# Context rows of the adaLN product moved from GpSimd to VectorE in the first stage of a hybrid attention layer

## The chip, the cores and the metric

The kernel runs on one core of a Trainium2 chip. The metric is the device time of one execution in microseconds (us); before the change it is 1164.74 us, the median of three runs (1163.18 to 1165.64). Lower is better.

## What is computed

One layer of a backbone over 1024 image tokens of width 1024, with 256 context tokens in front of them. What matters here is the start of it, cut from the reference:

```python
def modulate(x, cond, norm_g, w_ada, b_ada):
    shift, scale, gate = jnp.split(jax.nn.silu(cond) @ w_ada + b_ada, 3, axis=-1)
    ...
    return rms_norm(x, norm_g) * (1 + scale) + shift, gate

h, gate = modulate(x, c, lp['norm_g'], lp['w_ada'], lp['b_ada'])
hc, gate_c = modulate(xc, c_ctx, lp['norm_g'], lp['w_ada'], lp['b_ada'])
z = h @ lp['w_in']
kc, vc = na_kv(hc @ lp['w_in'][:, A_K:A_Z], lp['k_norm_g'])
```

So shift and scale are products of a vector (silu of the condition) with the 1024 x 1024 matrices of `w_ada`, once with the image's condition and once with the context's. Behind it come the projections of `z`, neighbourhood attention with context keys, two convolution branches, gates, and the output projection. Everything is float32; each matmul is made of three products of high and low parts.

## The kernel before, in words

The first stage walks over eight columns k of 128 channels. Tiles of 128 tokens of x (`xt`, 128 x 1024) are normed row by row (`normed`, L312 to L320: squares with a sum on ScalarE, the root on GpSimd by `rsqrt_mean`, L77 and L78, the scaling at L319 on VectorE). Tiles 0 to 3 are the first half of the image (`ha`, one tile per column), tiles 4 and 5 and later 6 and 7 the second half (`hb`); two context tiles follow.

For a column k the two rows of `w_ada` (scale and shift, 128 x 1024, 512 KB each) are loaded on SyncE's queue (`load_w_ada`, L300) and each is multiplied with the row of silu(c) and summed by one VectorE instruction (`image_ada`, L351, instruction at L355). Two tiny instructions then give the column's scale A (L357) and shift B (L358). In `modulated` (L322) TensorE transposes the tiles (L327), ScalarE writes the high part with A and B applied (L329) and the same value in full (`xh`, L332), and a subtraction makes the low part (L335). `outer` (L378) multiplies the column at once with the first weights of q, k and v, into six PSUM banks: L380 and L381 need the high part, L382 the low part. `second` (L386) does a column of tiles 4 and 5, three columns behind the first half (`LAG = 3`). `rest_image` (L420) does tiles 6 and 7; their products run inside `qkv` by `mm3` (L106 to L108). After that come the first gate (`glu_steps`, tile `gps`) and the context.

The same 16 rows of `w_ada` are needed with silu(c_ctx): `ctx_ada(i)`, L360, i = 2 x column + (0 scale, 1 shift). In the kernel before, rows 0 to 7 are done in two pieces inside the column loop: GpSimd multiplies (L368) and ScalarE sums (L370). Rows 8 to 15 are single VectorE instructions (L366), emitted behind the loop. The tables `W_POOL`, `LO_POOL` and `LO_POOL2` say which low parts of weights (`split_chunk`, L89) and of columns (L335) GpSimd makes. A scheduler orders the instructions of each engine; `tc.issue_after` holds a piece back until another one. Each engine then works its list in order.

`row4k` is a ring of 14 buffers (`ROWS`) of 4 KB per partition, for x tiles from number 3 on, `w_ada` rows from 6 on, the silu(c_ctx) row `sc1` and later weights; a load into it waits for the last reader of the buffer it reuses.

Of the kernel before, what the change touches and what calls it, by code (L numbers as in the profile page):

```python
# [8 lines left out]
F32 = mybir.dt.float32  # L9
F32R = mybir.dt.float32r  # L10
BF16 = mybir.dt.bfloat16
AF = mybir.ActivationFunctionType
ALU = mybir.AluOpType
# [4 lines left out]
P = 128  # L18
D = 1024
KT = 8  # L20
S = 1024
# [6 lines left out]
MASK_PAD = 1024  # L28
WARM = 10
NT = 2  # L30
ROWS = 14
LAG = 3
EARLY = 6
RAW1 = 6
CTX_AT = (8, 3, 3, 3)

LO_POOL, LO_POOL2, W_POOL = (7,), (4, 5, 6, 7), (0, 1, 2, 4, 5, 6)

CTX_ROWS = {0: 1, 1: 2, 2: 3, 3: 4, 4: 5, 5: 6, 6: 7, 7: 7}


@with_exitstack
def tile_hybrid(ctx: ExitStack, tc, x, xT, cx, cond, crow, ng, w_ada, b_ada, wqkv, wz,
                wout, wo, qg, kg, rpbs, mask, cs, cf, cfb, lng, lnb, out):
    nc = tc.nc
    pe, act, dve, pool = nc.tensor, nc.scalar, nc.vector, nc.gpsimd
# [22 lines left out]
    def const(src, shape, name):  # L69
        t = cst.tile(shape, F32, name=name)  # L70
        nc.sync.dma_start(t, src)
        return t


    def rsqrt_mean(dst, ss, n, k):

        pool.tensor_scalar(out=dst, in0=ss, scalar1=1.0 / n, scalar2=EPS, op0=ALU.mult, op1=ALU.add)  # L77
        pool.tensor_tensor(out=dst, in0=dst, in1=half_neg[:, :k], op=ALU.pow)  # L78


    def split_chunk(src, n, lo_eng, raw=None):
        wp = state["wp"]
        if raw is None:
            raw = wp.tile([P, 384], F32, tag="wr", name="wr", bufs=3)
            nc.sync.dma_start(raw[:, :n], src)
        hi = wp.tile([P, 384], F32R, tag="wh", name="wh")
        act.copy(hi[:, :n], raw[:, :n])  # L87
        lo = wp.tile([P, 384], F32R, tag="wl", name="wl")
        state["lo"] = lo_eng.tensor_tensor(out=lo[:, :n], in0=raw[:, :n], in1=hi[:, :n].bitcast(F32), op=ALU.subtract)  # L89
        return hi, lo  # L90

    def load_w(src, kts, lo_eng):
# [31 lines left out]
    B512 = [slice(0, 512), slice(512, 1024)]  # L124
    state = {"wp": wp}
# [103 lines left out]
    def hcols(part, k, sl):  # L229

        o = sl.start // 512
        return hlf[o][k][:, part, sl.start - o * 512 : sl.stop - o * 512]
    chd = dram.tile([KT, P, 2 * L], F32, name="chd")

    def tmp(name="tmp"):
        return rp.tile([P, 512], F32, tag="tmp", name=name)
# [29 lines left out]
    with tc.tile_pool(name="st", bufs=1) as st, tc.tile_pool(name="ps_t", bufs=1, space=PSUM) as pst:  # L266
# [6 lines left out]
        def row4k(name, dt=F32):  # L273
            return st.tile([P, D], dt, tag="row", name=name, bufs=ROWS)

        def four(t):
            return t.rearrange("p (a b n) -> p a b n", a=2, b=2)
# [9 lines left out]

        def silu_rows(i):

            r = row4k("sc1") if i else st.tile([P, D], F32, name="sc")  # L290
            for h in range(2):
                ps = pst.tile([P, 512], F32, tag="t", name="c_ps", bufs=NT)
                for k in range(4):
                    pe.transpose(out=ps[:, k * P : k * P + P], in_=cond_t[:, 4 * h + k, i : i + 1].broadcast_to([P, P]), identity=ident)
                if i:
                    act.copy(r[:, B512[h]], ps)
                else:
                    dve.tensor_copy(r[:, B512[h]], ps)
            return four(r)

        def load_w_ada(k):
            ws = []
            for j in (1, 0):
                w = four(hp_pool.tile([P, D], F32, tag=f"hb{7 - 2 * k - j}", name="wada") if 2 * k + j < EARLY else row4k("wada"))
                nc.sync.dma_start(w, four(w_ada[j, k]))
                ws.append(w)
            return ws

        def load_x(src, t, x_):
            nc.sync.dma_start(x_, four(src[t * P : (t + 1) * P, :]))  # L310
            return x_

        def normed(xt, eng=dve):
            sq = st.tile([P, 2, 2, 256], BF16, tag="sq", name="sq")
            ss = st.tile([P, 1], F32, tag="ss", name="ss", bufs=2)
            act.activation(sq, xt, AF.Square, accum_out=ss)
            rs = st.tile([P, 1], F32, tag="rs", name="rs", bufs=2)
            rsqrt_mean(rs, ss, D, 1)
            eng.tensor_scalar(out=xt, in0=xt, scalar1=rs, scalar2=None, op0=ALU.mult)  # L319
            return xt  # L320

        def modulated(k, tiles, i, hi, lo, on=act, sub=dve):  # L322

            n = len(tiles) * P
            pt = pst.tile([P, 512], F32, tag="t", name="xT_ps", bufs=NT)
            for j, xt in enumerate(tiles):
                pe.transpose(out=pt[:, j * P : (j + 1) * P], in_=xt[:, k // 4, k % 4 // 2, k % 2 * P : k % 2 * P + P], identity=ident)  # L327
            a, b = A_t[:, k, i : i + 1], B_t[:, k, i : i + 1]
            act.activation(hi, pt[:, :n], AF.Identity, bias=b, scale=a)  # L329
            xh = st.tile([P, 512], F32, tag="xh", name="xh", bufs=3)  # L330
            if on is act:
                act.activation(xh[:, :n], pt[:, :n], AF.Identity, bias=b, scale=a)  # L332
            else:
                dve.tensor_scalar(out=xh[:, :n], in0=pt[:, :n], scalar1=a, scalar2=b, op0=ALU.mult, op1=ALU.add)
            sub.tensor_tensor(out=lo, in0=xh[:, :n], in1=hi.bitcast(F32), op=ALU.subtract)  # L335

        sc = silu_rows(0)
# [4 lines left out]
        x0 = [load_x(x, t, four(a1.tile([P, D], F32, tag=("qT", "kT", "vb")[t], name="xt")) if t < 3 else four(row4k("xt"))) for t in range(4)]  # L342
        wa = [load_w_ada(0)]
        scx = silu_rows(1)
# [3 lines left out]
        dx = st.tile([P, KT, 2], F32, name="dx")  # L348
        w0 = []
# [10 lines left out]
        def ctx_ada(i):  # L360

            k, j = i // 2, i % 2
            w, d = wa[k][j], dx[:, k, j : j + 1]
            if i not in CTX_ROWS:
                junk = st.tile([P, 2, 2, 256], BF16, tag="junk", name="junk", bufs=1)
                dve.scalar_tensor_tensor(out=junk, in0=w, scalar=1.0, in1=scx, op0=ALU.mult, op1=ALU.mult, accum_out=d)  # L366
            else:
                pool.tensor_tensor(out=w, in0=w, in1=scx, op=ALU.mult)  # L368
                sq = st.tile([P, 2, 2, 256], BF16, tag="sq", name="sq")
                act.activation(sq, w, AF.Identity, accum_out=d)  # L370

        image_ada(0)
        for xt in x0:
            normed(xt)
        x1, lo_ins = [], []

        def outer(k, ts):
            for t in ts:  # L378
# [6 lines left out]

        def second(k):  # L386
            hlf[1].append(hp_pool.tile([P, 2, 512], F32R, tag=f"hb{k}", name=f"hb{k}"))
            modulated(k, x1, 0, hcols(0, k, slice(512, 768)), hcols(1, k, slice(512, 768)), act, (dve, pool)[k in LO_POOL2])
            outer(k, (4, 5))

        for k in range(KT):
            raw = tmp("wraw")[:, :384]
            nc.sync.dma_start(raw, wqkv[0, :, k * 384 : k * 384 + 384])
            w0.append(split_chunk(None, 384, (dve, pool)[k in W_POOL], raw))
            if k:
                wa.append(load_w_ada(k))
                image_ada(k)
            modulated(k, x0, 0, hcols(0, k, B512[0]), hcols(1, k, B512[0]), act, (dve, pool)[k in LO_POOL])
            outer(k, range(4))
            lo_ins.append(state["lo"].ins)  # L400
            with tc.issue_after(lo_ins[-1]):
                for i in range(2 * KT):
                    if CTX_ROWS.get(i) == k:
                        ctx_ada(i)
            if k == 1:
                x1 += [normed(load_x(x, t, four(row4k("xt")))) for t in (4, 5)]
            if k >= LAG:
                second(k - LAG)
        for k in range(KT - LAG, KT):
            second(k)  # L410
        with tc.issue_after(state["ada"].ins):
            for i in range(2 * KT):
                if i not in CTX_ROWS:
                    ctx_ada(i)
        qg_t = const(qg, [P, 1], "qg_t")
        kg_t = const(kg, [P, 1], "kg_t")
        dve.tensor_scalar(out=qg8, in0=qg_t, scalar1=HD ** -0.5, scalar2=None, op0=ALU.mult)
        dve.tensor_scalar(out=kgn, in0=kg_t, scalar1=-1.0, scalar2=None, op0=ALU.mult)

        def rest_image():  # L420
            x1 = [normed(load_x(x, t, four(row4k("xt")))) for t in (6, 7)]
            for k in range(KT):
                modulated(k, x1, 0, hcols(0, k, slice(768, S)), hcols(1, k, slice(768, S)), (act, dve)[k % 4 > 0])

        rest_image()
        xc = [normed(load_x(cx, t, four(row4k("xt"))), (dve, pool)[t]) for t in range(2)]
        pool.tensor_tensor(out=A_t[:, :, 1], in0=dx[:, :, 0], in1=b1, op=ALU.add)
        pool.tensor_tensor(out=A_t[:, :, 1], in0=A_t[:, :, 1], in1=ng_t, op=ALU.mult)
        pool.tensor_tensor(out=B_t[:, :, 1], in0=dx[:, :, 1], in1=b_t[:, :8], op=ALU.add)
# [27 lines left out]
        for k in range(0, RAW1, 2):  # L457
            r = row4k("w1raw")
# [8 lines left out]
    with tc.tile_pool(name="at", bufs=1, reuse_waits="tile") as at, \  # L467
# [4 lines left out]
        for hf in range(2):  # L472
            m = mka[:, hf]
            for i in range(3):
                o, n = TYPE_OFF[i], (288, 384, 288)[i]
# [5 lines left out]
        for h in range(2):  # L481
            t = at.tile([P, S], F32R, name=f"qlz{h}")
# [3 lines left out]
        for i in range(4):  # L486
            t = at.tile([P, 768], F32, name=f"pbuf{i}")
# [683 lines left out]
    for dm in range(KT):  # L1171
        wr = wq.tile([P, D], F32, tag="wr", name="wrf", bufs=3)
        nc.sync.dma_start(wr, wo[dm])
        w = [x for h in range(2) for x in cut(wsplit(wr[:, B512[h]], (dve, pool)[h]))]
# [93 lines left out]
```

## Time and profile before

| | |
|---|---|
| median of three runs | 1164.74 us |
| the profiled execution's own time | 1165.39 us |
| its span in the trace | 1163.4 us |
| TensorE busy | 1112.9 us (96%) |
| VectorE busy | 841.9 us (72%) |
| GpSimd busy | 666.7 us (57%) |
| ScalarE busy | 556.6 us (48%) |
| mean granted TensorE clock | 0.978 of full |

The profiled execution took 2.0 us more than its span and 0.65 us more than the median. TensorE is busy for 90% or more of each of the 40 slices of the span (29 us each) but the first two, which have 6 and 7 tenths, and the third, with 7: what lies ahead of about 90 us is another kind of stage than all that follows.

### The profile page before, as it was taken

The page shows a single profiled execution, that of the slowest core. Times are in us where ns is not written, and L with a number is a line of the kernel's source. Part 1 is how long each engine was busy: PE and PEld are TensorE (multiplying, and loading weights), DVE is VectorE, ACT ScalarE, POOL GpSimd, SP SyncE. Part 2 cuts the span into 40 slices and gives each one's busy share as a digit, 9 for nine tenths or more (in the row PEclk, how much of TensorE's full clock was granted, in tenths as well). Part 3 has the DMA queues.
Part 4 walks back from the last instruction along what each step waited for, and adds up shares of the span by engine and source line. Part 5 has one row for each costly group of instructions (what it writes and reads, how often), then busy time and mean ns, then how long its engine had stood idle before and what let it go on. Part 6 is the DMA issues. An engine that isn't in the chain of part 4 may idle for free. (4 is left out here: it accounts for less than half of the span.)

```text
span 1163.4 us, 16409 instructions
## 1 busy us (share of the span) xinstructions
PE 1112.9 (96%) x5554; PEld 953.3 (82%) x5554; DVE 841.9 (72%) x1479; ACT 556.6 (48%) x1135; POOL 666.7 (57%) x607
## 2 busy tenths in 40 slices
PE   6779899999999999999999999999999999999998
PEld 4668798799899878887788888888888788878787
DVE  7995557787877886654899599699794476579311
ACT  5585357556746768876523232423334443523100
POOL 7676735645745873330677777778678462981100
PEclk6689999999999999999999999999999999999999
DMA  9344332332322242213524342534445983465421
GB/s 355 119 140 155 99 100 82 109 98 79 110 76 65 79 141 101 86 53 125 229 73 151 103 142 76 181 100 129 162 132 187 386 316 109 145 212 188 152 83 53
DMA packets 77779, 159.44 MB, mean 137 GB/s; under 512 B 9856, under 2 KB 29056, under 8 KB 77696
## 3 DMA queue, kind: packets, MB, share of 16 engines
q1 hardware_dynamic: 73088, 156.31, 39.7%
q10 hardware_dynamic: 4608, 2.10, 0.6%
q8 instruction: 43, 0.70, 0.3%
q14 instruction: 40, 0.33, 0.1%
HBM read 116.43 MB, written 41.94 MB: 136 GB/s over the span
## 5 line engine op out<-in xcount | busy, mean ns | idle before, releaser
L698 DVE SCALAR_TENSOR_TENSOR cv<-upad,cf_t,cv 128x512 f32<-128x512 f32 x240 | 167.1, 747 | 0.1
L536 POOL TENSOR_TENSOR bias<-mka,vimg 128x288 f32<-128x288 bf16 (+1 forms) x64 | 56.6, 884 | 87.3 <-DVE mn L550 79.2
L89 POOL TENSOR_TENSOR wl<-wr,wh 128x384 fp32r<-128x384 f32 (+1 forms) x57 | 56.8, 1001 | 54.1 <-ACT wh L87 42.4
L646 POOL TENSOR_TENSOR wl<-s,wh 128x512 fp32r<-128x512 f32 x57 | 79.2, 1403 | 12.4 <-ACT wh L645 11.7
L645 ACT CAST wh<-s 128x512 fp32r<-128x512 f32 x76 | 46.1, 616 | 77.5 <-POOL s L649 65.8
L572 DVE TENSOR_TENSOR plo<-pp,ph 128x512 fp32r<-128x512 f32 (+1 forms) x96 | 60.6, 639 | 8.1 <-ACT ph L570 7.5
L552 ACT ACTIVATE pbuf<-sc,mn 128x256 f32<-128x256 f32 x64 | 30.4, 475 | 73.6 <-DVE mn L550 73.3
L567 PE MATMUL pp<-ident,pbuf 128*128 128x128 f32 x352 | 59.0, 274 | 4.1 <-DVE pbuf L556 2.8
L646 POOL TENSOR_TENSOR wl<-wr,wh 128x512 fp32r<-128x512 f32 x44 | 60.5, 1375 | 4.2 <-ACT wh L645 4.2
L722 PE MATMUL ga<-ha,wh 128*128 128x512 f32 x152 | 59.3, 390 | 1.2 <-ACT wh L645 1.2
L724 PE MATMUL ga<-ha,wl 128*128 128x512 f32 x152 | 59.2, 389 | 0.0
L723 PE MATMUL ga<-ha,wh 128*128 128x512 f32 x152 | 59.2, 389 | 0.0
L570 ACT CAST ph<-pp 128x512 fp32r<-128x512 f32 (+1 forms) x96 | 51.5, 548 | 15.5 <-PE pp L567 14.9
L554 DVE TENSOR_TENSOR mn<-mn 128x1 f32<-128x1 f32 x64 | 18.8, 295 | 51.9 <-ACT pbuf L553 51.5
L1182 DVE SCALAR_TENSOR_TENSOR o<-fin,gate,xr 128x512 f32<-128x512 f32 x16 | 12.0, 751 | 58.0 <-PE fin L108 58.0
L106 PE MATMUL fin<-mh,wh 128*128 128x512 f32 x128 | 50.0, 390 | 1.4 <-ACT mh L645 1.4
L567 PEld LDWEIGHTS pp<-ident,pbuf 128*128 128x128 f32 x352 | 42.6, 140 | 10.2 <-DVE pbuf L556 5.2
L646 POOL TENSOR_TENSOR wl<-wrf,wh 128x512 fp32r<-128x512 f32 x8 | 12.6, 1574 | 65.2 <-ACT wh L645 56.8
L108 PE MATMUL fin<-mh,wl 128*128 128x512 f32 x128 | 49.9, 390 | 0.0
L107 PE MATMUL fin<-ml,wh 128*128 128x512 f32 x128 | 49.8, 389 | 0.0
L750 POOL TENSOR_TENSOR s<-wr 128x512 f32<-128x512 f32 x16 | 23.2, 1448 | 38.9 <-DMA wr<-in_wz 38.8
L78 POOL TENSOR_TENSOR ssh<-ssh,half_neg 128x4 f32<-128x4 f32 (+1 forms) x40 | 39.5, 990 | 2.7
(393 smaller groups left out, 4040.6 us busy)
## 6 DMA issues: line engine op xcount, KB each, us to landing
wr<-in_wz SPq DMA_DIRECT2D x34, 512.0 KB, 3.9
gs<-gd SPq DMA_DIRECT2D x24, 512.0 KB, 5.3
wada<-in_w_ada SPq DMA_DIRECT2D x16, 512.0 KB, 8.7
wr<-in_wz SPq DMA_DIRECT2D x36, 192.0 KB, 2.4
cht<-chd SPq DMA_DIRECT2D x24, 256.0 KB, 3.0
wro<-in_wout SPq DMA_DIRECT2D x24, 256.0 KB, 4.7
gd<-gate SPq DMA_DIRECT2D x22, 256.0 KB, 3.6
vimg<-in_rpbs SPq DMA_DIRECT2D x16, 288.0 KB, 3.0
```

The costliest lines, as they stand in the source:

```text
L89: state["lo"] = lo_eng.tensor_tensor(out=lo[:, :n], in0=raw[:, :n], in1=hi[:, :n].bitcast(F32), op=ALU.subtract)
L106: pe.matmul(ps, ah, bh, start=i == 0, stop=False)
L108: pe.matmul(ps, al, bh, start=False, stop=i == n - 1)
L536: pool.tensor_tensor(out=bv, in0=mv, in1=iv, op=ALU.subtract)
L567: pe.transpose(out=pp[:, c * 256 + hf * P : c * 256 + hf * P + P], in_=pts[hf][:, o : o + P], identity=ident)
L570: act.copy(ph[:, : m * 256], pp[:, : m * 256])
L572: dve.tensor_tensor(out=plo[:, : m * 256], in0=pp[:, : m * 256], in1=ph[:, : m * 256].bitcast(F32), op=ALU.subtract)
L646: eng.tensor_tensor(out=lo, in0=src, in1=hi.bitcast(F32), op=ALU.subtract)
L698: dve.scalar_tensor_tensor(out=acc[b], in0=src, scalar=cf_t[:, i, j : j + 1], in1=acc[b], op0=ALU.mult, op1=ALU.add)
L722: pe.matmul(ps, wh, bh, start=first and j == 0, stop=False, skip_group_check=True)
L723: pe.matmul(ps, wh, bl, start=False, stop=False, skip_group_check=True)
L724: pe.matmul(ps, wl, bh, start=False, stop=last and j == 3, skip_group_check=True)
```

## The change

All 16 context rows become single VectorE instructions. Six of them (rows 5, 4, 3 in the columns 4, 5, 6, and rows 2, 1, 0 in column 7) are emitted in the column loop, held back until the column's image rows are done; the other ten are emitted one or two at a time behind the columns of `rest_image`. GpSimd makes no more low parts there: those of the weights and of all columns of the image are VectorE's. The tiles 4 to 7 of x and the second context tile are scaled by ScalarE (`act.activation` with a scale) and no longer by VectorE or GpSimd. In `rest_image` the full value is written by VectorE in four columns of eight, where it was six. The ring has 13 buffers, since `sc1` has its own now.

```diff
-ROWS = 14
+ROWS = 13
-LO_POOL, LO_POOL2, W_POOL = (7,), (4, 5, 6, 7), (0, 1, 2, 4, 5, 6)
-CTX_ROWS = {0: 1, 1: 2, 2: 3, 3: 4, 4: 5, 5: 6, 6: 7, 7: 7}
+CTX_ROWS = {5: 4, 4: 5, 3: 6, 2: 7, 1: 7, 0: 7}
...
-            r = row4k("sc1") if i else st.tile([P, D], F32, name="sc")
+            r = st.tile([P, D], F32, name=("sc", "sc1")[i])
...
-            eng.tensor_scalar(out=xt, in0=xt, scalar1=rs, scalar2=None, op0=ALU.mult)
+            if eng is act:
+                act.activation(xt, xt, AF.Identity, scale=rs)
+            else:
+                eng.tensor_scalar(out=xt, in0=xt, scalar1=rs, scalar2=None, op0=ALU.mult)
...
-            w, d = wa[k][j], dx[:, k, j : j + 1]
-            if i not in CTX_ROWS:
-                junk = st.tile([P, 2, 2, 256], BF16, tag="junk", name="junk", bufs=1)
-                dve.scalar_tensor_tensor(out=junk, in0=w, scalar=1.0, in1=scx, op0=ALU.mult, op1=ALU.mult, accum_out=d)
-            else:
-                pool.tensor_tensor(out=w, in0=w, in1=scx, op=ALU.mult)
-                sq = st.tile([P, 2, 2, 256], BF16, tag="sq", name="sq")
-                act.activation(sq, w, AF.Identity, accum_out=d)
+            junk = st.tile([P, 2, 2, 256], BF16, tag="junk", name="junk", bufs=1)
+            dve.scalar_tensor_tensor(out=junk, in0=wa[k][j], scalar=1.0, in1=scx, op0=ALU.mult, op1=ALU.mult, accum_out=dx[:, k, j : j + 1])
...
-            modulated(k, x1, 0, hcols(0, k, slice(512, 768)), hcols(1, k, slice(512, 768)), act, (dve, pool)[k in LO_POOL2])
+            modulated(k, x1, 0, hcols(0, k, slice(512, 768)), hcols(1, k, slice(512, 768)))
...
-            w0.append(split_chunk(None, 384, (dve, pool)[k in W_POOL], raw))
+            w0.append(split_chunk(None, 384, dve, raw))
...
-            modulated(k, x0, 0, hcols(0, k, B512[0]), hcols(1, k, B512[0]), act, (dve, pool)[k in LO_POOL])
+            modulated(k, x0, 0, hcols(0, k, B512[0]), hcols(1, k, B512[0]))
...
-            with tc.issue_after(lo_ins[-1]):
-                for i in range(2 * KT):
-                    if CTX_ROWS.get(i) == k:
+            with tc.issue_after(state["ada"].ins):
+                for i in CTX_ROWS:
+                    if CTX_ROWS[i] == k:
                         ctx_ada(i)
             if k == 1:
-                x1 += [normed(load_x(x, t, four(row4k("xt")))) for t in (4, 5)]
+                x1 += [normed(load_x(x, t, four(row4k("xt"))), act) for t in (4, 5)]
...
-        with tc.issue_after(state["ada"].ins):
-            for i in range(2 * KT):
-                if i not in CTX_ROWS:
-                    ctx_ada(i)
+        late = [i ^ 1 for i in range(2 * KT) if i ^ 1 not in CTX_ROWS]
...
         def rest_image():
-            x1 = [normed(load_x(x, t, four(row4k("xt")))) for t in (6, 7)]
+            x1 = [normed(load_x(x, t, four(row4k("xt"))), act) for t in (6, 7)]
             for k in range(KT):
-                modulated(k, x1, 0, hcols(0, k, slice(768, S)), hcols(1, k, slice(768, S)), (act, dve)[k % 4 > 0])
+                modulated(k, x1, 0, hcols(0, k, slice(768, S)), hcols(1, k, slice(768, S)), (act, dve)[k % 2])
+                with tc.issue_after(state["ada"].ins):
+                    for i in late[: 1 + k % 2]:
+                        ctx_ada(late.pop(0))
...
-        xc = [normed(load_x(cx, t, four(row4k("xt"))), (dve, pool)[t]) for t in range(2)]
+        xc = [normed(load_x(cx, t, four(row4k("xt"))), (dve, act)[t]) for t in range(2)]
```

Since a scheduler sets the order, two places are shown as the engines' lists have them. The first is VectorE from column 4 to column 6 of the loop. `junk,da` is an image row, `junk,dx` a context row, `ha_171` and `ha_172` are the first half's columns 4 and 5, `hb_...` columns of tiles 4 and 5, `wl` a low part of a weight. Before:

```order
L335 TENSOR_TENSOR ha_171<-xh,ha_171 128x512
L358 TENSOR_SCALAR B_t<-da,b_t 128x1
L355 SCALAR_TENSOR_TENSOR junk,da<-wada,sc 128x1024
L335 TENSOR_TENSOR hb_509<-xh,hb_509 128x256
L355 SCALAR_TENSOR_TENSOR junk,da<-wada,sc 128x1024
L357 TENSOR_SCALAR A_t<-da,b_222,ng_t 128x1
L335 TENSOR_TENSOR ha_172<-xh,ha_172 128x512
L358 TENSOR_SCALAR B_t<-da,b_t 128x1
```

Now (the lines have moved by one or two):

```order
L356 SCALAR_TENSOR_TENSOR junk,da<-wada,sc 128x1024
L336 TENSOR_TENSOR ha_171<-xh,ha_171 128x512
L336 TENSOR_TENSOR hb_499<-xh,hb_499 128x256
L356 SCALAR_TENSOR_TENSOR junk,da<-wada,sc 128x1024
L358 TENSOR_SCALAR A_t<-da,b_222,ng_t 128x1
L87 TENSOR_TENSOR wl<-wraw,wh 128x384
L359 TENSOR_SCALAR B_t<-da,b_t 128x1
L365 SCALAR_TENSOR_TENSOR junk,dx<-wada,sc_236 128x1024
L87 TENSOR_TENSOR wl<-wraw,wh 128x384
L356 SCALAR_TENSOR_TENSOR junk,da<-wada,sc 128x1024
L336 TENSOR_TENSOR ha_172<-xh,ha_172 128x512
```

A context row and low parts of weights stand on VectorE between two columns now, where only the image's work stood.

The second is ScalarE at the end of the loop. `ha_174` is column 7 of the first half; `sq,ss<-xt` takes the squares of a tile of x (first tile 6, then tile 7); the `hb_` tiles are the columns 4 to 7 of tiles 4 and 5; the words in brackets are the semaphores that an instruction waits on. Before:

```order
L329 ACTIVATE ha_174<-xT_ps,B_t,A_t 128x512 [waits DVE_49,PE_49]
L332 ACTIVATE xh<-xT_ps,B_t,A_t 128x512
L370 ACTIVATE sq,dx<-wada 128x1024 [waits Activation_49]
L329 ACTIVATE hb_674<-xT_ps,B_t,A_t 128x256 [waits PE_49]
L332 ACTIVATE xh<-xT_ps,B_t,A_t 128x256
L316 ACTIVATE sq,ss<-xt 128x1024 [waits DMAHW3_49,Activation_49]
L329 ACTIVATE hb_688<-xT_ps,B_t,A_t 128x256 [waits PE_49]
```

Now:

```order
L330 ACTIVATE ha_174<-xT_ps,B_t,A_t 128x512 [waits DVE_49,PE_49]
L333 ACTIVATE xh<-xT_ps,B_t,A_t 128x512 [waits Activation_49]
L314 ACTIVATE sq,ss<-xt 128x1024 [waits DMAHW3_49]
L330 ACTIVATE hb_662<-xT_ps,B_t,A_t 128x256 [waits DVE_49,PE_49]
L333 ACTIVATE xh<-xT_ps,B_t,A_t 128x256 [waits Activation_49]
L330 ACTIVATE hb_676<-xT_ps,B_t,A_t 128x256 [waits DMAHW4_49,PE_49]
L333 ACTIVATE xh<-xT_ps,B_t,A_t 128x256 [waits Activation_49]
L318 ACTIVATE xt<-xt,rs 128x1024 [waits Activation_49,Pool_49]
```

The squares of tile 6, which wait for its load, stand ahead of the last four columns of tiles 4 and 5, and the scaling of tile 6 stands among them.

## Rows read from the trace of the kernel before

**Rows 1.** Windows: us; busy PE, PEld, DVE, ACT, POOL (x instructions); PEclk, DMA share, GB/s.

```profile
14.90:64.20 49.30, 35.00 (x133) 29.82 (x133) 47.40 (x64) 25.78 (x45) 35.01 (x17) 0.66 0.51 189
...
81.60:94.40 12.80, 12.29 (x78) 11.54 (x77) 11.17 (x26) 9.42 (x22) 11.01 (x15) 0.98 0.07 21
94.40:123.70 29.30, 29.30 (x162) 25.16 (x160) 12.42 (x21) 11.70 (x25) 13.48 (x17) 1.00 0.58 189
123.70:160.00 36.30, 30.86 (x175) 29.26 (x174) 21.27 (x39) 16.39 (x43) 23.52 (x30) 0.91 0.37 107
```

**Rows 2.** Waits, 14 to 64 us: who waited for whom, us in total, times, longest.

```profile
ACT ha L329 <- DVE B_t L358: 19.4, 5, 7.0
```

**Rows 3.** Grouped instructions, VectorE, 14.9 to 64.2 us: count | busy us, mean ns | idle before.

```profile
L355 DVE SCALAR_TENSOR_TENSOR junk<-wada,sc 128x1024 bf16<-128x1024 f32 x15 | 30.5, 2034 | 0.1
L335 DVE TENSOR_TENSOR ha<-xh,ha 128x512 fp32r<-128x512 f32 x7 | 5.4, 769 | 1.0 <-ACT xh L332 0.9
L319 DVE TENSOR_SCALAR xt<-xt,rs 128x1024 f32<-128x1024 f32 x3 | 5.0, 1682 | 1.4 <-POOL rs L78 1.4
L335 DVE TENSOR_TENSOR hb<-xh,hb 128x256 fp32r<-128x256 f32 x3 | 3.4, 1138 | 0.0
```

**Rows 4.** Timeline, VectorE: start us, us, instruction, idle before.

```profile
17.13 3.13 DVE L355 SCALAR_TENSOR_TENSOR junk<-wada,sc 128x1024 bf16<-128x1024 f32 x1
...
29.35 0.68 DVE L335 TENSOR_TENSOR ha<-xh,ha 128x512 fp32r<-128x512 f32 x1
29.96 0.55 DVE L89 TENSOR_TENSOR wl<-wraw,wh 128x384 fp32r<-128x384 f32 x1
...
42.86 3.25 DVE L355 SCALAR_TENSOR_TENSOR junk<-wada,sc 128x1024 bf16<-128x1024 f32 x1
...
62.87 0.41 DVE L335 TENSOR_TENSOR hb<-xh,hb 128x256 fp32r<-128x256 f32 x1
...
64.11 1.21 DVE L366 SCALAR_TENSOR_TENSOR junk<-wada,sc 128x1024 bf16<-128x1024 f32 x1
...
75.95 0.75 DVE L319 TENSOR_SCALAR xt<-xt,rs 128x1024 f32<-128x1024 f32 x1
...
90.54 0.42 DVE L335 TENSOR_TENSOR hb<-xh,hb 128x256 fp32r<-128x256 f32 x1
```

**Rows 5.** Timeline, GpSimd.

```profile
15.83 3.33 POOL L368 TENSOR_TENSOR wada<-wada,sc 128x1024 f32<-128x1024 f32 x1
...
38.40 6.63 POOL L368 TENSOR_TENSOR wada<-wada,sc 128x1024 f32<-128x1024 f32 x2
...
89.61 2.21 POOL L78 TENSOR_TENSOR ssh<-ssh,half_neg 128x4 f32<-128x4 f32 x2
```

**Rows 6.** Windows, two shorter stretches, columns as in rows 1.

```profile
14.90:38.00 23.10, 15.11 (x48) 12.69 (x48) 21.36 (x26) 11.07 (x19) 18.83 (x11) 0.57 1.03 395
38.00:50.00 12.00, 7.03 (x22) 5.55 (x22) 11.97 (x12) 3.92 (x7) 11.73 (x5) 0.64 0.03 3
```

**Rows 7.** Timeline, TensorE.

```profile
30.09 1.65 PE L382 MATMUL ps<-wh,ha 128*128 128x384 f32 x4 [0.96 <-DVE ha L335]
...
34.35 0.99 PE L382 MATMUL ps<-wh,ha 128*128 128x384 f32 x4
37.64 0.33 PE L327 MATMUL xT_ps<-ident,xt 128*128 128x128 f32 x1 [2.31 <-DVE xt L319]
...
61.62 0.60 PE L327 MATMUL xT_ps<-ident,xt 128*128 128x128 f32 x4
...
94.38 0.48 PE L106 MATMUL gps<-ha,ghi 128*128 128x512 f32 x1
```

**Rows 8.** Grouped instructions, VectorE, 64.1 to 94.4 us.

```profile
L366 DVE SCALAR_TENSOR_TENSOR junk<-wada,sc 128x1024 bf16<-128x1024 f32 x8 | 11.1, 1390 | 0.1
```

**Rows 9.** Timeline, ScalarE: the squares of tile 6.

```profile
67.69 1.07 ACT L316 ACTIVATE sq<-xt 128x1024 bf16<-128x1024 f32 x1
```

**Rows 10.** DMA issues, 62 to 66 us: count, KB each, median us from issue to landing.

```profile
xt<-in_x SPq DMA_DIRECT2D x2, 512.0 KB, 3.4
```

More of the change, by code (lines that the diff above doesn't have):

```diff
@@ L88, in split_chunk @@
         lo = wp.tile([P, 384], F32R, tag="wl", name="wl")
-        state["lo"] = lo_eng.tensor_tensor(out=lo[:, :n], in0=raw[:, :n], in1=hi[:, :n].bitcast(F32), op=ALU.subtract)
+        lo_eng.tensor_tensor(out=lo[:, :n], in0=raw[:, :n], in1=hi[:, :n].bitcast(F32), op=ALU.subtract)
         return hi, lo
@@ L374, in tile_hybrid @@
             normed(xt)
-        x1, lo_ins = [], []
+        x1 = []
         def outer(k, ts):
@@ L397, in tile_hybrid @@
                 image_ada(k)
-            modulated(k, x0, 0, hcols(0, k, B512[0]), hcols(1, k, B512[0]), act, (dve, pool)[k in LO_POOL])
+            modulated(k, x0, 0, hcols(0, k, B512[0]), hcols(1, k, B512[0]))
             outer(k, range(4))
-            lo_ins.append(state["lo"].ins)
-            with tc.issue_after(lo_ins[-1]):
-                for i in range(2 * KT):
-                    if CTX_ROWS.get(i) == k:
+            with tc.issue_after(state["ada"].ins):
+                for i in CTX_ROWS:
+                    if CTX_ROWS[i] == k:
                         ctx_ada(i)
             if k == 1:
-                x1 += [normed(load_x(x, t, four(row4k("xt")))) for t in (4, 5)]
+                x1 += [normed(load_x(x, t, four(row4k("xt"))), act) for t in (4, 5)]
             if k >= LAG:
```

## The prediction

> **What bounds the kernel now.** I read the windows first, then the waits, then the groups and the timelines of the engines that the waits name. From 94.4 to 123.7 us TensorE is busy all the time at the full clock, and nearly so from 81.6 on [rows 1]; the page shows the same to the end. So whatever lets the work at 94.4 (the first gate, `gps` [rows 7]) start earlier should move the end by as much. The stage ahead is different: from 14.9 to 64.2 us TensorE is busy 35.0 us of 49.3 at 0.66 of the clock, while VectorE is busy 47.4 [rows 1]. The waits say who holds whom: ScalarE waits 19.4 us for B, the last tiny VectorE instruction of a column [rows 2], and TensorE waits for ScalarE. **VectorE bounds the loop.**
>
> Its time there goes to the image rows: 15 instructions, 30.5 us, 2.03 us each [rows 3]. The same shape takes 1.21 us at 64.11 [rows 4]. What stretches them? Lay the two timelines side by side: the row of 17.13 took 3.13 us and began inside a GpSimd product that ran from 15.83 to 19.16; the one of 42.86 took 3.25 inside two products that ran from 38.40 to 45.03 [rows 4, 5]. Take the end of the GpSimd product and add 1.21: 20.37 and 46.24; the rows ended at 20.26 and 46.11. The VectorE row stood until GpSimd was through and then ran at its own speed. Loads are not the cause, since DMA moves 3 GB/s from 38 to 50 us [rows 6].
>
> **The change, part by part.**
>
> *Loop, VectorE, 14.9 to 64.2 us.* Taken away: the stretch of 15 image rows, 30.5 - 15 x 1.21 = 12.4 us. Scaling of tiles goes to ScalarE, or (tile 3) is no longer stretched: of 5.0 us in three instructions one of 0.75 stays, so 4.3, and 1.4 of waits for the root ahead of two of them [rows 3, 4]. Low parts of columns run unstretched: seven of the first half 5.4 - 7 x 0.68 = 0.6, and of the second half four at 0.41 in place of three in 3.4 us, 1.8 [rows 3, 4]. Together 20.5. Added: eight low parts of weights at 0.55, 4.4 (two are there already, stretched; I count six, 3.3, and leave their stretch as reserve), and two more context rows, 2.4 [rows 4]. That is 20.5 - 5.7 = 14.8. Bounds: if GpSimd were not the cause, the first term is 0 and the sum 2.4; the best is 14.8 plus that reserve, some 16. I take **14**, close to the upper end, because every slow row that I laid beside GpSimd fits the sum above within 0.2 us. The rest is held back for three new waits: the low part of column 1 stands directly behind B of that column, so VectorE waits for ScalarE's two reads; the rows of column 2 come behind tiles 4 and 5 on SyncE's queue, 2 x 512 KB at 395 GB/s, 2.7 us [rows 6], of which most is slack; and ScalarE, in order, stands at the squares of tile 6.
>
> *That last wait, and who is behind it.* The load of tile 6 waits for TensorE's transposes of column 7 (61.62 now [rows 7], about 50 then), lands 3.4 us later [rows 10], and only then come its squares (1.07 us [rows 9]) and the columns 4 to 7 of tiles 4 and 5. Tile 7's load waits for the transposes of the last of these. Two loads in a row, 2 x 3.4, and two squares: bounds for the cost are 0 (VectorE has the context rows to do meanwhile) and 4.5 (load and squares bare).
>
> *Behind the loop, VectorE, 64.2 to 94.4 us.* Here it does eight context rows in 11.1 us [rows 8]; in the change three of the 16 are done by B of column 7, so 13 follow, 13 x 1.21 = 15.7: plus 4.6. GpSimd's five low parts, 0.68 + 4 x 0.41 = 2.3, come over; one low part has gone ahead, minus 0.4; two tiles are scaled by ScalarE, minus 1.5 [rows 4]. Sum **+5.0**. Two full values of a column also leave VectorE, which I do not count.
>
> *ScalarE* loses eight sums and gains five scalings of 128x1024. No row shows such a scaling: between VectorE's 0.75 and the square's 1.07 [rows 4, 9]; I take 1.07, 5.4 us in all. It costs nothing while ScalarE is busy 25.8 of 49.3 us [rows 1]; without that cover two scalings of tiles 6 and 7, 2.1, would lie on the path. *GpSimd* keeps only roots. Do they stretch VectorE as the products did? The low part of 90.54 took 0.42 us beside two roots of 128x4 that ran from 89.61 to 91.82 [rows 4, 5], as short as elsewhere: 0. The Trainium skill (SBUF — State Buffer, Who interferes with whom) states that a VectorE instruction with two SBUF inputs and a GpSimd instruction that reads SBUF exclude one another, the later one standing until the earlier is done. By it each of some 16 roots left could hold VectorE once, for at most half of that 2.21 us, and the sum would lose up to 17 us; the long products agree with the page, this row does not show it for roots, and the row decides.
>
> *Sum.* 14 - 5 = **9.0 us** earlier at `gps`, 85.4 in place of 94.4. TensorE's 29.3 us without a gap [rows 1] carry it on; in the next stretch TensorE idles 5.4 of 36.3 us [rows 1], on waits that hang on work of the same stage, which moves along. The profiled execution took 1165.39 us: 1165.39 - 9.0 = 1156.4. The median is 0.65 lower: **1155.7 us**. A measurement of this kernel tells about 0.2%, 2.3 us, from no change.
>
> **The rivals.**
>
> *All of it arrives.* The reserve in the loop and the uncounted full values come through, no new wait shows: 16 - 5 + 2 = 13 us, 1152. For it: all stretched instructions are gone at once. Against it: an order with this many engines in a ring seldom has no wait.
>
> *Part is given back.* ScalarE's stand at tile 6 costs its upper bound, 4.5 us: 1160. For it: the list of ScalarE shows it plainly. Against it: VectorE has six context rows to do there, 7.3 us.
>
> *TensorE at its low clock becomes the bound: no change.* Four products of a low part took 1.65 us at 30.09 (1.2 GHz) and 0.99 at 34.35, when TensorE had been busy without a gap since 30.09; after the idle 2.31 us behind it the clock was down again [rows 7]. In the stage the mean is 0.57 to 0.66 [rows 1, 6]. If it stays at 1.2 GHz, a column with 18 products of at most 0.41 each and six transposes costs about 7 us of TensorE. VectorE's share of a column is 5.7: three rows of 1.21, 0.68, 0.41, 0.55 and the two tiny ones. Over eight columns the loop ends some 10 us later than I have it, and the gain is gone: 1165. Against it: a TensorE that bounds has no gaps, and without gaps the clock rose. The Trainium skill (TensorE: Matmul & The Clock Gate, HAM oscillation — how this bites in real kernels) says that work in bursts with idle time between them starts each burst at the low clock again; the row of 37.64 agrees.
>
> *Slower: tile 7 comes too late.* Place: ScalarE at the end of the loop. Each of the two loads in a row is kept back, since the transposes that free their buffers wait for PSUM that ScalarE reads, and the four context rows left when tile 7 is scaled (4.8 us) then lie between VectorE's low parts and TensorE. It decides from the point where tile 7 is scaled later than now, at 76.70 [rows 4]: that needs 11 us of delay against my course. Then the time is today's plus 4.8, less what rows 8 save when their slow instance goes, 1: about 1168. For it: the order allows it. Against it: 11 us is more than both loads and squares, 8.9, together.
>
> *The change does not do what it says:* the stretch is VectorE's own for rows fresh from DMA. Then the first sum is 2.4 and the result 2.6 us slower, 1167; the idle DMA at 42.86 speaks against it. I put it with the slower case.
>
> **How the numbers follow.** Forecast with its own range 1152.5 to 1159: 0.60. All of it: 0.10. Part given back: 0.14. No change by the clock: 0.08. Slower: 0.08. So faster by over 0.2% has 0.84, within 0.2% 0.08, slower 0.08. The range reaches from the best case with its bounds, 1150, to 1163, into the clock's case; outside are the slower case and most of that one.
>
> **What would show it.** Right: image rows at 1.2 us throughout; B of column 7 near 50 us; `gps` near 85; the same gap-free 29 us of TensorE behind it. Wrong: rows above 2 us without GpSimd beside them; TensorE busy without gaps at 0.5 of the clock in the loop; tile 7 scaled after 70; or `gps` early and the gain lost between 115 and 150 us. I would be wrong in kind if the stage behind 123.7 us waited on something that does not move along, a load issued at a fixed place in SyncE's queue for one.

## The result and the profile after

| | before | after |
|---|---|---|
| median, runs beside each other | 1164.92 us (4 runs, 1163.18 to 1165.64) | 1153.58 us (4 runs, 1152.51 to 1156.59) |
| profiled execution | 1165.39 us | 1156.59 us |
| its span | 1163.4 us | 1153.8 us |

The ratio is 0.9909 (95% interval 0.9887 to 0.9931): faster by about 1%. The forecast was 1155.7 us within 1150 to 1163. The profiled execution is the slowest of the four after, so it shows 8.8 us where the medians show 11.3. Five more runs of the same kernel on another chip gave 1154.87 us beside 1164.57, 9.7 us less (below, as `again`); 9 to 11 us is the honest size of the gain.

The windows of after, with the columns of [rows 1]; the fourth and the fifth are as long as the gap-free stretch of before and the one behind it.

```profile
14.90:51.00 36.10, 29.09 (x146) 27.13 (x146) 34.07 (x75) 22.01 (x36) 2.46 (x4) 0.82 0.71 265
51.00:64.00 13.00, 7.87 (x45) 6.56 (x43) 11.52 (x22) 11.05 (x23) 3.93 (x7) 1.00 0.59 215
64.00:84.00 20.00, 15.41 (x79) 13.77 (x77) 16.05 (x37) 13.67 (x29) 13.15 (x18) 0.74 0.15 52
85.50:114.80 29.30, 29.30 (x159) 25.27 (x157) 12.14 (x20) 11.27 (x27) 12.66 (x15) 1.00 0.60 196
114.80:151.10 36.30, 32.06 (x191) 30.37 (x191) 22.80 (x47) 17.47 (x46) 25.56 (x36) 0.95 0.33 103
```

The column loop, 49.3 us long before, takes 34.6 to the end of B of column 7; the first window goes 1.5 us beyond it. GpSimd is busy 2.46 us there instead of 35.01 [rows 1]. Grouped instructions of VectorE in that stretch (count | busy us, mean ns | idle before):

```profile
L356 DVE SCALAR_TENSOR_TENSOR junk<-wada,sc 128x1024 bf16<-128x1024 f32 x15 | 18.3, 1220 | 0.1
L365 DVE SCALAR_TENSOR_TENSOR junk<-wada,sc 128x1024 bf16<-128x1024 f32 x5 | 6.1, 1219 | 0.0
L336 DVE TENSOR_TENSOR ha<-xh,ha 128x512 fp32r<-128x512 f32 x7 | 4.8, 686 | 1.6 <-ACT xh L333 1.6
L87 DVE TENSOR_TENSOR wl<-wraw,wh 128x384 fp32r<-128x384 f32 x8 | 4.3, 553 | 0.2 <-ACT wh L85 0.2
L336 DVE TENSOR_TENSOR hb<-xh,hb 128x256 fp32r<-128x256 f32 x4 | 1.7, 417 | 0.0
```

The same 15 image rows went from 2034 to 1220 ns, and the low parts from 769 to 686 and from 1138 to 417 [rows 3]. The waits of 14 to 64 us answer to [rows 2]:

```profile
ACT ha L330 <- DVE B_t L359: 9.5, 6, 3.1
```

19.4 us became 9.5. Then the marks: B of the last column on VectorE's timeline, before and in the change, and the first gate on TensorE's.

```profile
63.99 0.20 DVE L358 TENSOR_SCALAR B_t<-da,b_t 128x1 f32<-128x1 f32 x1
```

```profile
49.26 0.21 DVE L359 TENSOR_SCALAR B_t<-da,b_t 128x1 f32<-128x1 f32 x1
```

```profile
85.50 0.50 PE L104 MATMUL gps<-ha,ghi 128*128 128x512 f32 x1
```

B of column 7 comes 14.7 us earlier, the gate 8.9 us earlier (94.38 [rows 7]). From there the traces run alike: 1069.0 us from gate to end before, 1068.3 after. So 5.9 us are given back between the loop and the gate, and nothing behind it.

### The profile page after: what moved, and what is told of

It reads as the page before. It is cut to its first block, busy times and chain, and to the rows that moved or that the text cites. A ratio compares the mean times of both kernels' runs of the same rounds, so it can differ in the third digit from the quotient of the medians.

```text
span 1153.8 us, 16402 instructions
## 1 busy us (share of the span) xinstructions
PE 1109.0 (96%) x5554; PEld 950.2 (82%) x5554; DVE 828.1 (72%) x1500; ACT 553.4 (48%) x1126; POOL 623.2 (54%) x587
## 5 line engine op out<-in xcount | busy, mean ns | idle before, releaser
L546 ACT ACTIVATE pbuf<-sc,mn 128x256 f32<-128x256 f32 x64 | 30.4, 475 | 71.9 <-DVE mn L544 71.6
L104 PE MATMUL ps<-wh,hb 128*128 128x384 f32 x112 | 40.0, 357 | 2.9 <-ACT hb L330 2.9
```

The costliest lines, as they stand in the source:

```text
L104: pe.matmul(ps, ah, bh, start=i == 0, stop=False)
```

## The experiments

Each group of runs has its own time of the kernel before, on the same chip. Context rows in two pieces, the context rows alone, the low parts and both scalings at once ran beside 1165.41 us; the added products, the fills and the first ring of 14 beside 1164.32; the repeat of the change, the second ring of 14 and the single scalings beside 1164.57.

### Context rows in two pieces again

```diff
-CTX_ROWS = {5: 4, 4: 5, 3: 6, 2: 7, 1: 7, 0: 7}
+CTX_ROWS = {0: 1, 1: 2, 2: 3, 3: 4, 4: 5, 5: 6, 6: 7, 7: 7}
...
+            if i in CTX_ROWS:
+                pool.tensor_tensor(out=wa[k][j], in0=wa[k][j], in1=scx, op=ALU.mult)
+                sq = st.tile([P, 2, 2, 256], BF16, tag="sq", name="sq")
+                act.activation(sq, wa[k][j], AF.Identity, accum_out=dx[:, k, j : j + 1])
+                return
```

> The changed kernel with one part undone: context rows 0 to 7 are again a GpSimd product and a ScalarE sum, one per column as before; low parts and scalings stay as in the change. Theory (a GpSimd product that reads SBUF holds up the VectorE row beside it until it is done): eight products of about 3.3 us stretch image rows again, mean 1.8 to 2.0 us each in the loop, B of column 7 falls back from 49 us to 57 to 61, and the time goes from 1153.6 to 1159 to 1163. Rival (the gain came from the low parts and the scalings, or from another order): rows near 1.2 us, B of column 7 before 52, time within 1.5 us of 1153.6.

Measured: 1157.64 us, ratio 0.9940 (0.9923 to 0.9956). The eight products alone bring a stretch back, though less on the image rows than the expected 1.8 to 2.0 us: part of it falls on the low parts that VectorE makes now (in the change 686 ns for the first half, 553 for the weights). VectorE's groups, 14.9 to 66.5 us:

```profile
L356 DVE SCALAR_TENSOR_TENSOR junk<-wada,sc 128x1024 bf16<-128x1024 f32 x15 | 22.3, 1484 | 0.0
L336 DVE TENSOR_TENSOR ha<-xh,ha 128x512 fp32r<-128x512 f32 x8 | 9.9, 1235 | 1.6 <-ACT xh L333 1.6
L87 DVE TENSOR_TENSOR wl<-wraw,wh 128x384 fp32r<-128x384 f32 x8 | 8.6, 1089 | 0.0
```

B of column 7 stands at 60.22, in the expected span and 11 us later than in the change; the gate only 4.4 later (89.88): eight context rows follow on VectorE there and not 13. So the time is less than expected.

### The context rows alone

The kernel before, with rows 0 to 7 as single VectorE instructions and nothing else changed:

```diff
-            if i not in CTX_ROWS:
-                junk = st.tile([P, 2, 2, 256], BF16, tag="junk", name="junk", bufs=1)
-                dve.scalar_tensor_tensor(out=junk, in0=w, scalar=1.0, in1=scx, op0=ALU.mult, op1=ALU.mult, accum_out=d)
-            else:
...
+            junk = st.tile([P, 2, 2, 256], BF16, tag="junk", name="junk", bufs=1)
+            dve.scalar_tensor_tensor(out=junk, in0=w, scalar=1.0, in1=scx, op0=ALU.mult, op1=ALU.mult, accum_out=d)
```

> The kernel before with one part of the change alone: context rows 0 to 7 as single VectorE instructions at the same columns; low parts and scalings stay where they were. Theory: VectorE gets eight rows of 1.22 us more in the loop, 9.8, and loses the stretch of its 15 image rows, 12.4, less what the low parts on GpSimd still cost; B of column 7 at 58 to 62 us (64 before). Behind the loop nothing changes on VectorE. Time 1158 to 1163, so only part of the gain: the late place of ten rows carries the rest. Rival (who does the rows is all that matters): 1153 to 1156.

Measured: 1157.85 us (10 runs), ratio 0.9946 (0.9931 to 0.9961), just under what was expected; B of column 7 at 54.11, earlier than expected. This part alone brings more than half of the gain. The rest of the stretch stays: GpSimd still makes low parts, and image rows have a mean of 1301 ns. TensorE then waits for tile 4 to 7's low parts (waits, 51 to 92 us):

```profile
PE ps L108 <- DVE hb L335: 5.2, 2, 4.7
PE ps L377 <- POOL hb L335: 3.5, 3, 1.9
```

### Low parts on GpSimd again

```diff
+LO_POOL, LO_POOL2, W_POOL = (7,), (4, 5, 6, 7), (0, 1, 2, 4, 5, 6)
...
-            modulated(k, x1, 0, hcols(0, k, slice(512, 768)), hcols(1, k, slice(512, 768)))
+            modulated(k, x1, 0, hcols(0, k, slice(512, 768)), hcols(1, k, slice(512, 768)), act, (dve, pool)[k in LO_POOL2])
...
-            w0.append(split_chunk(None, 384, dve, raw))
+            w0.append(split_chunk(None, 384, (dve, pool)[k in W_POOL], raw))
```

(and the same with `LO_POOL` for the first half)

> The changed kernel with the low parts of six weights and five columns on GpSimd again (products stay away). Theory: they are GpSimd instructions that read SBUF too, 0.7 to 2 us each, and each holds up the VectorE instruction beside it for a part of that; VectorE saves 3.3 us for the weights in return. In the loop these nearly cancel (B of column 7 at 48 to 51 us); the columns' low parts come later. Time 1154 to 1157. Rival (the low parts were the larger part of the gain): 1159 or more.

Measured: 1158.76 us, ratio 0.9944 (0.9928 to 0.9961): a miss, the cost is some 2 to 5 us more than expected. B of column 7 stands at 51.33, 2.1 us later than in the change; the rest comes behind the loop. Small GpSimd subtractions stretch VectorE's rows too (1301 and 1398 ns), and are stretched by them. Both show in the groups of 14.9 to 66.5 us on VectorE and of 14.9 to 85 on GpSimd:

```profile
L357 DVE SCALAR_TENSOR_TENSOR junk<-wada,sc 128x1024 bf16<-128x1024 f32 x15 | 19.5, 1301 | 0.1
L366 DVE SCALAR_TENSOR_TENSOR junk<-wada,sc 128x1024 bf16<-128x1024 f32 x12 | 16.8, 1398 | 0.2
```

```profile
L337 POOL TENSOR_TENSOR hb<-xh,hb 128x256 fp32r<-128x256 f32 x4 | 6.5, 1655 | 0.0
```

A low part of 0.42 us on VectorE takes 1.66 there. What I had left out is who waits for it: TensorE waits 2.3 us for GpSimd's `hb`, and 4.2 for tile 7, which is scaled at 68.26 instead of 62.53. The gate stands at 90.14.

### Eight products that nobody needs

The changed kernel, with eight GpSimd products added that read what the old ones read; their result is not read, and VectorE's list is unchanged:

```diff
+            if 3 <= k < 7:
+                gh = st.tile([P, 2, 2, 256], BF16, tag="gh", name="gh", bufs=1)
+                for j in range(2):
+                    pool.tensor_tensor(out=gh, in0=scx, in1=wa[k][j], op=ALU.mult)
```

> The changed kernel plus eight GpSimd products of 128x1024 (rows of columns 3 to 6 times the context row, into a tile that nobody reads), right behind the root of tile 5. Nothing waits for them but the buffers they read, which are needed again only after 60 us; VectorE's own list is unchanged. Theory (lock): from about 24 us on VectorE rows beside them take 2 to 3.3 us, each standing until the product is through; B of column 7 goes from 49 us to 58 to 65, and the time from 1153.6 to 1161 to 1167. Rival (the rows were slow because of the waits and ScalarE sums that hung on the products): rows at 1.2 us, time within 1.5 us of 1153.6.

Measured: 1170.95 us, ratio 1.0058 (1.0040 to 1.0075): slower than before, and beyond the upper end of what was expected. GpSimd's products ran back to back; its timeline, and VectorE's beside it:

```profile
24.70 23.55 POOL L398 TENSOR_TENSOR gh<-sc,wada 128x1024 bf16<-128x1024 f32 x8
```

```profile
28.07 0.20 DVE L359 TENSOR_SCALAR B_t<-da,b_t 128x1 f32<-128x1 f32 x1
28.19 2.59 DVE L87 TENSOR_TENSOR wl<-wraw,wh 128x384 fp32r<-128x384 f32 x1
30.70 3.36 DVE L356 SCALAR_TENSOR_TENSOR junk<-wada,sc 128x1024 bf16<-128x1024 f32 x1
...
33.99 2.81 DVE L336 TENSOR_TENSOR ha<-xh,ha 128x512 fp32r<-128x512 f32 x1
...
52.23 1.23 DVE L356 SCALAR_TENSOR_TENSOR junk<-wada,sc 128x1024 bf16<-128x1024 f32 x1
```

Every VectorE instruction with two large inputs that begins between 24.7 and 48.3 us takes about one product's time, whether it needs 0.55, 0.69 or 1.22 us alone; tiny ones of 128x1 keep their 0.20, and rows behind the products their 1.2. The groups close the account: image rows 26.7 us against 18.3, weights' low parts 10.5 against 4.3, the first half's 6.9 against 4.8. That is 16.7 us, and B of column 7 moved by 16.9 (66.18).

### The same bytes written, nothing read

In the same four columns, sixteen fills of the same tile, each pair behind a product of 128x1; nobody reads the tile:

```diff
+                    pool.tensor_tensor(out=gh[:, 0, 0, :1], in0=wa[k][j][:, 0, 0, :1], in1=scx[:, 0, 0, :1], op=ALU.mult)
+                    for _ in range(2):
+                        pool.memset(gh, 0.0)
```

> The same place with GpSimd instructions that only write: 16 memsets of the same 128x1024 tile, each pair behind a 128x1 product that ties it to the load of a row. Theory (it is the shared reading that locks): VectorE rows stay at 1.2 us beside the memsets, B of column 7 at 49 to 50 us, time within 1.5 us of 1153.6. Rival (any GpSimd instruction locks VectorE out): rows stretched wherever a memset runs, B of column 7 after 54, time 1158 or more.

Measured: 1154.94 us, ratio 0.9911 (0.9895 to 0.9928), as the changed kernel. GpSimd is busy 23.2 us between 14.9 and 51, and VectorE's image rows do not notice (timeline of GpSimd, group of VectorE):

```profile
35.50 1.96 POOL L400 MEMSET gh<- 128x1024 bf16 x2
```

```profile
L356 DVE SCALAR_TENSOR_TENSOR junk<-wada,sc 128x1024 bf16<-128x1024 f32 x15 | 18.3, 1218 | 0.1
```

So it is not a busy GpSimd that stretches VectorE, but a GpSimd that reads. The Trainium skill (SBUF — State Buffer, Who interferes with whom) states just this difference between a GpSimd instruction that reads SBUF and one that only writes; the two runs agree, 3.25 to 3.39 us against 1.22.

### Scalings back on VectorE and GpSimd

Tiles 4 to 7 scaled by VectorE, the second context tile by GpSimd; then each of the two alone (the first two lines, the last line).

```diff
-                x1 += [normed(load_x(x, t, four(row4k("xt"))), act) for t in (4, 5)]
+                x1 += [normed(load_x(x, t, four(row4k("xt")))) for t in (4, 5)]
...
-            x1 = [normed(load_x(x, t, four(row4k("xt"))), act) for t in (6, 7)]
+            x1 = [normed(load_x(x, t, four(row4k("xt")))) for t in (6, 7)]
...
-        xc = [normed(load_x(cx, t, four(row4k("xt"))), (dve, act)[t]) for t in range(2)]
+        xc = [normed(load_x(cx, t, four(row4k("xt"))), (dve, pool)[t]) for t in range(2)]
```

> The changed kernel with tiles 4 to 7 scaled by VectorE and the second context tile by GpSimd again. Theory: 4 scalings of 0.75 us on VectorE instead of 1.15 on ScalarE; VectorE is the bound in the loop, so two of them cost 1.5 us there, while the chain of tile 7 gets 0.4 us shorter. Time 1154 to 1156. Rival (ScalarE's scalings are what freed VectorE): 1158 or more.

> Changed kernel with tiles 4 to 7 of the image scaled on VectorE; the second context tile stays on ScalarE. The edit that undid both scalings lost 4.9 us though its gate stood at the same time. If VectorE's four extra 0.75 us (3 us, that end in later context rows) cost it: 1156 to 1158.5. If the GpSimd product of the context tile cost it: as the changed kernel, 1153 to 1155.

> Changed kernel with only the second context tile scaled by GpSimd (3.67 us where it was measured), tiles 4 to 7 on ScalarE. If that product cost the 4.9 us (it stands before the context's columns, and VectorE instructions beside it wait): 1156 to 1158.5. If VectorE's four scalings did: as the changed kernel, 1153 to 1155.

Measured: both 1158.53 us (0.9945, 0.9928 to 0.9962), a miss by 2.5; the image's tiles alone 1156.60 (0.9925, 0.9909 to 0.9942); the context tile alone 1154.67 (0.9911, 0.9894 to 0.9929). The 1158.53 lies in the range of the rival. The context tile's place shows no cost. VectorE's four scalings alone come to about 2 us, but their interval overlaps that of the change. What is lost is not lost ahead of the gate: it stands at 85.54 with both undone and at 83.54 with the image's alone (85.50 and 83.96 in the change), but from there to the end these two profiles take 1070.8 and 1071.4 us and not 1068.3. What is later is the context's scale on GpSimd, 77.0 us in the change, 81.5 and 81.1 in these two. Whether that is the cause was not tested.

### A ring of 14 again

```diff
-ROWS = 13
+ROWS = 14
```

> The changed kernel with a ring of 14 buffers instead of 13, so that the load of tile 6 finds a free buffer and goes out behind the rows of w_ada, and tile 7 takes tile 3's buffer, not tile 4's. Theory (the two loads in a row and ScalarE's stand at the squares of tile 6 are what lies between the loop and the rest): tile 7 is scaled at 58 to 60 us instead of 63.7, TensorE's idle 2.9 us ahead of its transposes is gone, the gate starts at 82 to 84 instead of 85.5, time 1150.5 to 1153. Rival (behind the loop VectorE's ten context rows and low parts bound, not the loads): the gate at 85 to 86, time within 1 us of 1153.6.

> The changed kernel, nothing edited, as the measure for the three beside it on the same chip. Theory (9 us at the first gate, carried to the end): 1153 to 1157, ratio .988 to .993. What is asked is its spread too: its profiled execution of before (1156.59) was the slowest of its four times.

> Ring of 14 again, against the changed kernel on one chip. Theory A (whatever starts the first gate earlier arrives at the end; the spread of the times hid it): 6 to 7 us under the changed kernel, 1147 to 1150. Rival B (part is given back behind the gate, since the context rows end at 76.2 there against 77.0 and do not move along): 2 to 3 us under it, 1150.5 to 1152.

Measured: first 1151.31 us, ratio 0.9881 (0.9866 to 0.9895), then beside the changed kernel on one chip 1149.70, 0.9870 (0.9852 to 0.9888), against 1154.87, 0.9907 (0.9890 to 0.9924). That is 5.2 us less than the change by the medians (4.3 by the ratios), in the range of theory A's times though short of its 6 to 7 us, and with no edit to the work: **the fastest version of this study, 14.9 us under the kernel before**. ScalarE's timeline shows where it comes from. The change, at the end of the loop (the squares of 52.06 are tile 6's, of 59.42 tile 7's):

```profile
52.06 1.06 ACT L314 ACTIVATE sq<-xt 128x1024 bf16<-128x1024 f32 x1 [1.05 <-DMA xt<-in_x]
...
54.91 1.16 ACT L318 ACTIVATE xt<-xt,rs 128x1024 f32<-128x1024 f32 x1
...
59.42 1.06 ACT L314 ACTIVATE sq<-xt 128x1024 bf16<-128x1024 f32 x1
...
62.53 1.15 ACT L318 ACTIVATE xt<-xt,rs 128x1024 f32<-128x1024 f32 x1 [0.67 <-POOL rs L76]
```

With 14 buffers, in the second of the two profiles (here tile 6 is already scaled at 45.39, and tile 7 squared at 52.90):

```profile
45.39 1.14 ACT L318 ACTIVATE xt<-xt,rs 128x1024 f32<-128x1024 f32 x1
...
52.90 1.06 ACT L314 ACTIVATE sq<-xt 128x1024 bf16<-128x1024 f32 x1 [0.89 <-DMA xt<-in_x]
...
55.95 1.18 ACT L318 ACTIVATE xt<-xt,rs 128x1024 f32<-128x1024 f32 x1
```

One tile fewer waits for a buffer: tile 7 is ready 6.6 us earlier. TensorE's waits of the change in 51 to 85 us begin with the two that this takes away (0.9 us of the second is left in the first profile with 14):

```profile
PE xT_ps L328 <- ACT xt L318: 2.9, 1, 2.9
PE ps L104 <- ACT hb L330: 2.9, 1, 2.9
```

The gate stands at 78.85 and 79.59 in the two profiles, earlier than the expected 82 to 84, against 85.50 and 83.96 for the change.

```profile
79.59 0.48 PE L104 MATMUL gps<-ha,ghi 128*128 128x512 f32 x1
```

From B of column 7 (49.3 in all four) to the gate that is 30 us, as many as in the kernel before (30.4), although 13 context rows follow there and not eight; why is told in the next section.

## Why the prediction came out

**The cause, right and shown.** The term of 12.4 us for stretched image rows measured 12.2 (30.5 to 18.3). That GpSimd's products are the cause was read from two rows [rows 4, 5]; the added products make it slower than before, and the fills leave it. The rival that the stretch is VectorE's own falls: beside the fills the same rows, as fresh from DMA, take 1218 ns.

**The loop, right.** I took 14 us, after 14.8 by the sum; B of column 7 moved by 14.7. The low parts went to 686, 417 and 553 ns, where I had put 0.68, 0.41 and 0.55 us. The wait held back for column 1 is there, 1.6 us on ScalarE's `xh`. Slips in the sum nearly cancel, as two rows of VectorE's timeline before show:

```profile
13.55 1.47 DVE L319 TENSOR_SCALAR xt<-xt,rs 128x1024 f32<-128x1024 f32 x1 [0.71 <-POOL rs L78]
...
58.94 2.74 DVE L89 TENSOR_TENSOR wl<-wraw,wh 128x384 fp32r<-128x384 f32 x1
```

Tile 3's scaling, and the wait ahead of it, lay ahead of the loop already, so the terms of 4.3 and 1.4 should be 3.6 and 0.7. Three context rows stand ahead of B of column 7, as the step behind the loop says, and not two: 1.2 us more. The weights' low parts, 4.3 us now, took 3.3 before (0.55 and this 2.74), so they add 1.0 and not 3.3. With that the sum is 14.5.

**Behind the loop, right in size, half wrong in its reason.** The step said +5.0 us, for work that VectorE does more. Given back were 5.9. The stretch from the end of B of column 7 to the gate shows what they were made of (columns of [rows 1]; in this order the kernel before, the change, and the two profiles with 14 buffers):

```profile
64.19:94.38 30.19, 24.28 (x134) 22.20 (x135) 27.38 (x51) 23.24 (x52) 25.20 (x28) 0.89 0.39 135
49.47:85.50 36.03, 25.69 (x137) 22.45 (x135) 29.90 (x63) 27.61 (x56) 17.31 (x25) 0.86 0.34 117
49.51:78.85 29.34, 22.45 (x130) 19.00 (x128) 28.61 (x61) 24.20 (x51) 13.57 (x22) 1.00 0.35 126
49.55:79.59 30.04, 25.37 (x132) 22.16 (x130) 28.62 (x61) 24.18 (x51) 13.77 (x22) 0.89 0.36 123
```

VectorE is busy 29.9 us there and not 27.4, so its work ahead of the gate grew by 2.5 us and not by 5.0. The step did not count the two full values that leave VectorE, nor all that had been stretched there before. The other 3.3 us VectorE stands idle: 6.1 us against 2.8. With 14 buffers it is idle for 0.7 and 1.4 us only, so there VectorE's work does fill the stretch, and the stretch is as long as in the kernel before. The idle time belongs to the other step, "that last wait, and who is behind it": I bounded ScalarE's stand at the loads of tiles 6 and 7 by 0 and 4.5, and set it at 0 but for what I held back in the loop. By the runs with 14 buffers it is worth 4.3 to 5.2 us at the end, about that upper bound, and the clock may add to it: behind TensorE's two waits of 2.9 us the granted clock is 0.74 from 64 to 84 us (windows above). From 50 to 76 us it is 0.80 in both profiles of the change, 1.00 and 0.87 in the two with 14 buffers. What the waits cost and what the clock, I did not separate. In that sense the rival "part is given back" held as well, and it is luck that the term I took for VectorE's work was as large as its work and the wait together. I saw the ring go from 14 to 13 and priced only what it delays, not that undoing it was free.

**The gate carries on to the end, right.** 29.30 us without a gap follow in both, and from gate to end the two differ by 0.7 us.

**The clock as the bound, fallen.** TensorE's granted clock in the loop rose from 0.66 to 0.82 and TensorE still waited there, for ScalarE's `ha` 7.0 us in four waits; here the stage that was fed faster had the higher clock. **Tile 7 too late, fallen:** it is scaled from 62.53 on, 13 us earlier than before (75.95 [rows 4]) and not later; the point from which it decides was not reached. **All of it arrives:** its 1152 is nearer to the median of four than my own number, but the repeat (1154.87) is not, and the wait it denied is there.

**Roots do not stretch VectorE, right.** From 64 to 84 us GpSimd is busy 13.15 us, most of it with roots, and in 51 to 85.5 us VectorE's context rows have a mean of 1222 ns, its low parts of 423. The up to 17 us that the rule of the Trainium skill (SBUF — State Buffer, Who interferes with whom) could have cost with roots do not show. Where one of the two stands, it is the root: see below.

## What to carry to other kernels

Before moving work between VectorE and GpSimd, look at the same shape in two places of the trace: if one instance ends just its own length after the end of a GpSimd instruction, then GpSimd's reading may cost VectorE time, and taking the work over can be cheaper for VectorE than leaving it. When an edit shortens one engine's list, price the loads that now come early against the buffers they wait for: here one buffer in a ring was worth nearly half as much as the whole change. And a sum that comes out is not yet proof of its terms; undo each part once.

## What the runs showed of the hardware

GpSimd seems to stand as well. Three roots on GpSimd's timeline in the change, and VectorE's instructions beside the second and the third:

```profile
64.75 0.55 POOL L76 TENSOR_TENSOR rs<-rs,half_neg 128x1 f32<-128x1 f32 x1
...
72.19 1.87 POOL L76 TENSOR_TENSOR ssh<-ssh,half_neg 128x4 f32<-128x4 f32 x1
...
79.48 1.01 POOL L76 TENSOR_TENSOR ssh<-ssh,half_neg 128x4 f32<-128x4 f32 x1
```

```profile
71.96 1.23 DVE L365 SCALAR_TENSOR_TENSOR junk<-wada,sc 128x1024 bf16<-128x1024 f32 x1
...
79.72 0.75 DVE L336 TENSOR_TENSOR hb<-xh,hb 128x256 fp32r<-128x256 f32 x2
```

The second root began inside the row and took 1.87 us; it ended 0.87 us behind the row, a little less than the 1.01 us that the third took in all. A root of 128x1 that began inside a row, at 60.93, took 1.57 us and not 0.55. In the other order nothing stands: the two low parts of 79.72 began inside the third root and ran in their own time. Why a root that has begun holds nothing, while a product does, no run here shows. VectorE in turn waits for such roots (5.8 us in five waits of 64 to 92 us, `tm` behind `ssh`); how much of that is what the roots lost before was not separated.

ScalarE takes 1.13 to 1.18 us to scale a tile of 128x1024 in place, VectorE 0.75; for the first no row of the kernel before had a price, and I had taken 1.07.

The same kernel's first gate stood at 85.50 in one execution and at 83.96 in another on a second chip, and times of one kernel spread over some 4 us: of a version that gains 5 us, one profile can show 3 or 7.
